# Weight tiles split in halves of their K tiles, with four half buffers, and token groups taken in the order of the K tiles

## The chip, the cores and the metric

The kernel runs on one core of one Trainium2 chip. The metric is the device time of one execution in microseconds (us), lower is better; the figure that counts is the median of several runs. The chance classes of the prediction go by 0.5%, since runs of one kernel differ by a few tenths of a per cent.

## The reference

The program is a decoder trunk with two residual layers over 512 tokens of width 2048, all in float32. Layer 0 is gated differential attention, layer 1 gated RWKV-7 time mixing.

```python
for i in range(2):                                  # layer 0, layer 1
    hn = rms_norm(x, norm_w[i])
    if i == 0:                                      # 8 heads, values of 256
        q, k, v, gate = split(hn @ da_w_in, 4)      # da_w_in 2048 x 8192
        o = causal_diff_attention(rope(rms(q)), rope(rms(k)), v, lam)
        out = (rms_norm(o) * (1 - lambda_init) * silu(gate)) @ da_w_out
    else:                                           # 32 heads of 64
        p = hn @ rw_w_in                            # 2048 x (4*2048 + 192)
        p = p + (token_shift(p) - p) * mu
        r, k, v, g, dw, da = split(p)
        y = wkv7_scan(r, decay(dw), k, v, a(da))    # S <- S*w + (S a) b + v k, y = S r
        out = (group_norm(y) + bonus) * silu(g) @ rw_w_out
    x = x + out
```

## The kernel before

**Arithmetic.** A matmul operand in float32 is split into a high part in the type float32r (a copy, which rounds) and a low part (the remainder), and a product is three matmuls: high by high, high by low, low by high (`mm3`, L114 to L119). The hidden states are held split for the whole layer (16 K tiles `hH`, `hL` of 128x512). The weights come from memory in groups: `load_w` (L73) puts 1024 columns per partition into a raw tile `wraw` (three buffers), and `split_w` (L88) makes `wh` with a copy on ScalarE (ACT, L104) and `wl` with a subtraction on VectorE (DVE, L105). `wh` and `wl` have two buffers each, so a third group can be split only when TensorE (PE) has done the last matmul of the first. `split_w` runs at a raised priority (`@urgent`).

**Layer 0.** `unit_tok` (L157) projects four blocks of 128 tokens by 512 columns: eight groups of KG = 2 K tiles, 24 matmuls in each, with the hidden states as stationary and the weights as moving operand. Within a group the order is token block by token block, save in groups marked `fine` (the first group of the kernel, whose split is also done K tile by K tile) and in a last group with work in `more`, which go K tile by K tile. The attention of the head before runs beside it in small steps (`Chain`, `tick`): after so many matmuls a step is put in. The output projections use `unit_tok` for two column blocks and then `seven` (L492), a Strassen-like form whose groups have 12 matmuls.

**Layer 1.** For each of 16 pairs of heads `unit_chan` (L883) projects one of k, g, r, v: two groups of KG = 8 K tiles by 128 columns (128x1024 again), 24 matmuls in each, K tile by K tile. So a pair takes eight groups, in the order v, k of the next pair, g of an earlier pair, r of the next pair. Three other things run beside these matmuls:

- the solve of a triangular system, `t_solve` (L1122): 31 steps of two dependent DVE instructions (`tmpl`, L1142, and `Tm`, L1144), from `LT` (L1133) to the last product (L1145); `Tm` then goes to memory and comes back as `TT` by two DMAs;
- `t_combine` (L1153): two DVE transposes of `TT` into `T1` (L1168, one per head; "T" in the profile), two runs of small matmuls `px` (L1174), copies to `X` (L1177), and two more runs of `px` (L1184). The matmuls `gp` of `gram` (L1075), whose copies to `G` (L1083) feed the next solve, stand between them;
- the scan, `scan_pair` (L1245): for each of 8 chunks a matmul `sm` (L1256), a copy to `rhs` on ACT (L1259), a matmul (L1267), a copy to `VS` on ACT (L1269), a matmul (L1274), and the next `VS` on DVE (L1278, in the first chunk L1281). Each step is put after a set number of projection matmuls.

**What sets the order.** The program is handed to a list scheduler (Tile), which fixes the order on every engine by priorities, by the set places of chain steps (`issue_after`) and by a model of durations. Engines then work strictly in that order: an instruction that waits holds up everything behind it on its engine. Buffers of a pool are taken in turn, so the scheduler also decides which instruction waits for which release.

Of the kernel before, what the change touches and what calls it, by code (L numbers as in the profile page):

```python
# [13 lines left out]
F32 = mybir.dt.float32  # L14
F32R = mybir.dt.float32r
# [8 lines left out]
P = 128  # L24
D = 2048
T = 512
KT = D // P
# [56 lines left out]
    return ld.ins  # L84


@urgent
def split_w(g, parts, kg, cols, k0, raw=None, fine=False, first=False):  # L88

    nc = g.nc  # L90
    if raw is None:
        raw = g.wraw.tile([P, kg, cols], F32, name="wraw", tag="wraw")
        load_w(g, raw, parts, k0, slice(0, kg))
    hi = g.wh.tile([P, kg, cols], F32R, name="wh", tag="wh")
    lo = g.wl.tile([P, kg, cols], F32R, name="wl", tag="wl")
    for ks in [slice(k, k + 1) for k in range(kg)] if fine else [slice(0, kg)]:
        k = k0 + ks.start
        with ExitStack() as after:
            if raw is not None and parts and k < 4:
                for ins in g.made[k - 1] if k else [g.made_prm]:  # L100
# [3 lines left out]
            nc.scalar.copy(hi[:, ks], raw[:, ks])  # L104
            nc.vector.tensor_sub(lo[:, ks], raw[:, ks], hi[:, ks].bitcast(F32))  # L105
    return hi, lo


def qk_cols(aps, h):
# [12 lines left out]
class Chain:  # L122
# [34 lines left out]
def unit_tok(g, aH, aL, parts, cols, npp=NT, more=None, late=True):  # L157

    nc = g.nc
    pts = [g.pp.tile([P, 512], F32, name="pp", tag="pp") if t < npp else  # L160
           g.ps.tile([P, 512], F32, name="pt", tag="pb", bufs=2) for t in range(NT)]
    KG = 1024 // cols
    m = None
    for k0 in range(0, KT, KG):
        raw, fine = g.first.pop(0) if g.first else (None, False)
        if fine:
            more(1, None)
        wh, wl = split_w(g, parts, KG, cols, k0, raw, fine)
        by_k = fine or more and late and k0 + KG == KT
        order = [(k, t) for k in range(KG) for t in range(NT)] if by_k else \  # L170
                [(k, t) for t in range(NT) for k in range(KG)]
        for i, (k, t) in enumerate(order):
            if more and (fine and i % 2 == 0 or i in (0, 2, 4)):
                more(1 + i // 2 if fine else k0 + (k + 1 + i % 4 // 2 if by_k else KG + i // 2), m)
# [267 lines left out]
class Rows:  # L442
# [5 lines left out]
    def __getitem__(self, k):  # L448
        return self.pairs[k][self.i]
# [3 lines left out]
KG = 2  # L453
# [143 lines left out]
def layer0(g, aps):  # L597
# [3 lines left out]
    with ExitStack() as cx:  # L601
# [46 lines left out]
        def more(n, m):  # L648
            for k in range(len(g.hH), min(n, KT)):
# [831 lines left out]
def body(ctx, tc, nc, aps):  # L1481
    g = Ctx()
# [42 lines left out]
```

## Time and profile before

| | us |
|---|---|
| median of 3 runs | 2230.39 |
| lowest and highest | 2227.97, 2237.57 |
| the profiled execution | 2223.03 |
| its span, first to last instruction | 2221.3 |
| PE busy | 2172.7 |
| DVE busy | 1405.4 |
| ACT busy | 1040.3 |

Layer 0 takes about the first 1000 us of the span, layer 1 the rest; the pairs of layer 1 run from about 1050 to 2050 us. The granted TensorE clock is full in every slice of the page. In the rows, "128x1024" is partitions by elements; a number in brackets is the idle time of the engine ahead of the instruction with what ended it; DVE, ACT and PE rows show starts that are exact and, for PE, ends that are modelled, so that on PE the distance from start to start says how long something took.

### The profile page before, as it was taken

To read this page: it belongs to the slowest core of one execution; us is meant where nothing else is said; L and a number is where in the kernel's file an instruction comes from. 1 tells how busy PE (TensorE), PEld (TensorE's weight loads), DVE (VectorE), ACT (ScalarE), POOL (GpSimd) and SP (SyncE) were. 2 spreads that over 40 slices of the span, in tenths; PEclk is the share of its full clock that TensorE was granted. 3 is DMA by queue.
4 is the path that set the end of the run, shared out by engine and by line. 5 is a ranking of instruction groups with operands and counts; after the bars stand their busy time and mean duration, and the time that the engine had idled before them with its cause. 6 is when DMAs were issued, how large, how long until landed. Compare 5 with 4: busy or idle time off the path is not lost.

```text
span 2221.3 us, 34087 instructions
## 1 busy us (share of the span) xinstructions
PE 2172.7 (98%) x12260; PEld 1754.3 (79%) x12260; DVE 1405.4 (63%) x3780; ACT 1040.3 (47%) x2118; POOL 300.3 (14%) x637
## 2 busy tenths in 40 slices
PE   9999999999999999999999999999999999999999
PEld 7888888888888888877767777777777777777887
DVE  5664636465564675475767677766667776667645
ACT  5443434344343454345555555555455555545322
POOL 0000000000000000111132212222222222231001
PEclk9999999999999999999999999999999999999999
DMA  6323232222323455644333323333333333345556
GB/s 191 97 84 97 76 105 89 92 95 77 99 82 97 145 190 194 161 108 108 86 77 77 91 75 93 83 79 91 91 91 82 87 86 77 98 136 185 170 165 121
DMA packets 296313, 240.21 MB, mean 108 GB/s; under 512 B 47792, under 2 KB 255680, under 8 KB 296144
## 3 DMA queue, kind: packets, MB, share of 16 engines
q1 hardware_dynamic: 256912, 190.13, 29.2%
q0 software_dynamic: 12384, 29.72, 6.2%
q10 hardware_dynamic: 26848, 18.18, 2.7%
q8 instruction: 97, 1.59, 0.3%
q14 instruction: 72, 0.59, 0.1%
HBM read 217.98 MB, written 19.99 MB: 107 GB/s over the span
## 4 chain that ended last, share of the span: by engine, by line
PE 70%; DVE 17%; ACT 4%; DMA 4%; issue 4%; POOL 0%; ACTq 0%; SPq 0%; DVEq 0%; POOLq 0%
PE pp L116 52%; PE pt L116 4%; DVE tmpl L1142 3%; DVE wl L105 3%; DMA td<-Tm 2%; DVE Tm L1144 2%; DMA TT<-td 1%; PE sc L116 1%; PE o L116 1%; PE sm L1267 1%; PE sm L1274 1%; DVE VS L1278 1%; PE sm L1256 1%; PE px L1174 1%; PE gp L1075 1%
## 5 line engine op out<-in xcount | busy, mean ns | idle before, releaser
L105 DVE TENSOR_TENSOR wl<-wraw,wh 128x1024 fp32r<-128x1024 f32 (+2 forms) x319 | 391.0, 1226 | 487.8 <-ACT wh L104 487.4
L104 ACT CAST wh<-wraw 128x1024 fp32r<-128x1024 f32 (+2 forms) x319 | 333.4, 1045 | 527.6 <-PE pp L116 387.9
L116 PE MATMUL pp<-wh,hH 128*128 128x512 f32 x1268 | 499.5, 394 | 0.5 <-ACT hH L869 0.3
L116 PE MATMUL pp<-wl,hH 128*128 128x512 f32 x1268 | 498.1, 393 | 0.0
L116 PE MATMUL pp<-wh,hL 128*128 128x512 f32 x1268 | 497.8, 393 | 0.1
L116 PE MATMUL pp<-hL,wh 128*128 128x512 f32 x1024 | 414.5, 405 | 0.0
L116 PE MATMUL pp<-hH,wl 128*128 128x512 f32 x1024 | 412.9, 403 | 0.0
L116 PE MATMUL pp<-hH,wh 128*128 128x512 f32 x1024 | 409.6, 400 | 0.0
L116 PEld LDWEIGHTS pp<-wh,hH 128*128 128x128 f32 x1268 | 238.3, 188 | 49.4 <-PE pp L116 0.6
L116 PEld LDWEIGHTS pp<-wh,hL 128*128 128x128 f32 x1268 | 238.2, 188 | 48.8 <-DVE hL L870 0.5
L116 PEld LDWEIGHTS pp<-wl,hH 128*128 128x128 f32 x1268 | 238.4, 188 | 46.6
L116 PEld LDWEIGHTS pp<-hH,wh 128*128 128x128 f32 x1024 | 193.1, 189 | 35.2 <-issue 1.8
L116 PEld LDWEIGHTS pp<-hL,wh 128*128 128x128 f32 x1024 | 193.1, 189 | 33.6
L116 PEld LDWEIGHTS pp<-hH,wl 128*128 128x128 f32 x1024 | 193.2, 189 | 31.9 <-issue 0.2
L1142 DVE SCALAR_TENSOR_TENSOR tmpl<-LT,Tm 128x60 f32<-128x60 f32 (+24 forms) x496 | 133.8, 270 | 9.8
L1262 POOL COPY SA<-VS 64x64 f32<-64x64 f32 x224 | 59.8, 267 | 418.3 <-DVE VS L1278 370.5
L462 POOL DMA_DIRECT2D frow<-yd x12 | 8.9, 744 | 794.4 <-DVE rs_t L67 675.1
L1144 DVE TENSOR_TENSOR Tm<-Tm,tmpl 128x60 f32<-128x60 f32 (+24 forms) x496 | 103.2, 208 | 8.0
L1259 ACT COPY rhs<-sm 64x64 f32<-64x64 f32 x256 | 52.9, 207 | 91.8 <-PE sm L1256 69.2
L1269 ACT COPY VS<-sm 64x64 f32<-64x64 f32 x256 | 52.9, 207 | 63.5 <-PE sm L1267 58.4
L1267 PEld LDWEIGHTS sm<-rhs,TT 128*128 128x128 f32 x256 | 41.8, 188 | 48.2 <-ACT rhs L1259 44.1
L1278 DVE SCALAR_TENSOR_TENSOR VS<-sm,gam,Sg 64x64 f32<-64x64 f32 x192 | 54.2, 282 | 31.6 <-PE sm L1274 27.2
(333 smaller groups left out, 3192.5 us busy)
## 6 DMA issues: line engine op xcount, KB each, us to landing
wraw<-in_rw_w_in_dram SPq DMA_DIRECT2D x128, 512.0 KB
wraw<-in_da_w_in_dram SPq DMA_DIRECT2D x254, 256.0 KB
wraw<-in_da_w_out_dram SPq DMA_DIRECT2D x26, 512.0 KB
wraw<-in_rw_w_out_dram SPq DMA_DIRECT2D x26, 512.0 KB
LT<-ltd POOLq DMA_DIRECT2D x64, 132.0 KB, 3.2
yr<-yd SPq DMA_DIRECT2D x28, 256.0 KB
frow<-yd POOLq DMA_DIRECT2D x12, 512.0 KB, 6.8
xq<-in_x_dram SPq DMA_DIRECT2D x16, 256.0 KB
```

Of the source, the lines that this page charges most:

```text
L104: nc.scalar.copy(hi[:, ks], raw[:, ks])
L105: nc.vector.tensor_sub(lo[:, ks], raw[:, ks], hi[:, ks].bitcast(F32))
L116: m = nc.tensor.matmul(out, a, b, start=s, stop=e, skip_group_check=skip)
L1075: m = nc.tensor.matmul(gp[h][:, i * P : (i + 1) * P], BK[r_, c0 + i, :, :], p.AR[r_, c0 + i, :, :], start=True, stop=True)
L1142: nc.vector.scalar_tensor_tensor(tt, LT[:, i : i + 1, i + 1 :].to_broadcast([P, s, n]), n2[:, i : i + 1], Tm[:, 0:s, i : i + 1].to_broadca ...
L1144: nc.vector.tensor_add(Tm[:, 0:s, i + 1 :], Tm[:, 0:s, i + 1 :], tt)
L1174: nc.tensor.matmul(px[hi, c * HALF : (c + 1) * HALF], p.G[lo, c, 0, h, HALF:C], T1[lo, c, :], start=True, stop=True, tile_position=(b0, b0 ...
L1259: nc.scalar.copy(rhs[r_, :], sm[r_, h * C : h * C + C])
L1262: nc.gpsimd.tensor_copy(p.SA[r_, c - 1, :], VS[r_, c, h, :])
L1267: nc.tensor.matmul(sm[:, P : P + C], both(g.TT[j % 2][:, c]), rhs[:], start=True, stop=True)
L1269: g.copied = nc.scalar.copy(VS[r_, c, h, :], sm[r_, P : P + C]).ins
L1278: g.state = nc.vector.scalar_tensor_tensor(VS[r_, c + 1, h, :], s_, p.gam[r_, c : c + 1], Sg[r_, :], ALU.mult, ALU.add)
```

## The change

`split_w` now makes two tiles of half the K tiles each instead of one (one K tile of 512 columns in layer 0, four K tiles of 128 columns in layer 1), each with its own copy and its own subtraction; a small class finds the right half when a matmul asks for K tile k. The pools `wh` and `wl` have four buffers of half the size in place of two, the same bytes. The middle groups of `unit_tok` (neither first nor last) go K tile by K tile. The old parameter `fine` of `split_w` goes, since every group is now split in halves; and the ties to the making of the first hidden states hold for the first loads alone. `wraw` and the loads are as before.

```diff
+class Halves:
+    def __init__(self, parts, n):
+        self.parts, self.n = parts, n
+    def __getitem__(self, at):
+        return self.parts[at[1] // self.n][at[0], at[1] % self.n, at[2]]
 
 @urgent
-def split_w(g, parts, kg, cols, k0, raw=None, fine=False, first=False):
+def split_w(g, parts, kg, cols, k0, raw=None, first=False):
...
-    hi = g.wh.tile([P, kg, cols], F32R, name="wh", tag="wh")
-    lo = g.wl.tile([P, kg, cols], F32R, name="wl", tag="wl")
-    for ks in [slice(k, k + 1) for k in range(kg)] if fine else [slice(0, kg)]:
-        k = k0 + ks.start
+    n = kg // 2
+    his, los = [], []
+    for k in range(0, kg, n):
+        hi = g.wh.tile([P, n, cols], F32R, name="wh", tag="wh")
+        lo = g.wl.tile([P, n, cols], F32R, name="wl", tag="wl")
...
-            nc.scalar.copy(hi[:, ks], raw[:, ks])
-            nc.vector.tensor_sub(lo[:, ks], raw[:, ks], hi[:, ks].bitcast(F32))
-    return hi, lo
+            nc.scalar.copy(hi[:], raw[:, k : k + n])
+            nc.vector.tensor_sub(lo[:], raw[:, k : k + n], hi[:].bitcast(F32))
+        his.append(hi)
+        los.append(lo)
+    return Halves(his, n), Halves(los, n)
...
-        by_k = fine or more and late and k0 + KG == KT
+        slow = more and late and k0 + KG == KT
+        by_k = fine or slow or 0 < k0 < KT - KG
...
-    g.wh = ctx.enter_context(tc.tile_pool(name="whp", bufs=2))
-    g.wl = ctx.enter_context(tc.tile_pool(name="wlp", bufs=2))
+    g.wh = ctx.enter_context(tc.tile_pool(name="whp", bufs=4))
+    g.wl = ctx.enter_context(tc.tile_pool(name="wlp", bufs=4))
```

The scheduler's order changes with it. On ACT and DVE 341 instructions each are added; PE, POOL and SP issue as many as before, POOL in the same order. Three places of a pair in the middle of layer 1 are shown (the order repeats from pair to pair there). The changed kernel's line numbers are 16 higher from L172 on, and its copy and subtraction stand at L117 and L118; a matmul on plain float32 counts once here and as two records in the profile.

On ACT, from the two scalings `BK` of the keys to a copy to `rhs` of the scan; before:

```order
L1038 ACTIVATE BK<-th_14966,prm_bk_b_1158,prm_bk_s_1155 128x8x64
L1259 COPY rhs<-sm 64x64 x2
L1038 ACTIVATE BK<-th_14966,prm_bk_b_1164,prm_bk_s_1161 128x8x64
L1028 ACTIVATE E<-m 128x8
L1269 COPY VS<-sm 64x64 x2
L1044 ACTIVATE k_15107<-mixk,prm_kk 128x512
L1029 ACTIVATE E<-l 128x8x64
L878 CAST sHx<-k_15107 128x512
L1030 ACTIVATE l<-l 128x512
L1214 COPY VS<-pt 64x4x64 x4
L104 CAST wh<-wraw 128x1024
L1259 COPY rhs<-sm 64x64 x2
```

And now, the same stretch:

```order
L1054 ACTIVATE BK<-th_15920,prm_bk_b_1228,prm_bk_s_1225 128x8x64
L1275 COPY rhs<-sm 64x64 x2
L117 CAST wh<-wraw 128x512
L1044 ACTIVATE E<-m 128x8
L1054 ACTIVATE BK<-th_15920,prm_bk_b_1234,prm_bk_s_1231 128x8x64
L1285 COPY VS<-sm 64x64 x2
L1045 ACTIVATE E<-l 128x8x64
L1060 ACTIVATE k_16069<-mixk,prm_kk 128x512
L1046 ACTIVATE l<-l 128x512
L894 CAST sHx<-k_16069 128x512
L1230 COPY VS<-pt 64x4x64 x4
L117 CAST wh<-wraw 128x512
```

The next row of the changed kernel is the same copy to `rhs` (L1275), with another half behind it. The whole group that stood ahead of that copy has become one half ahead of it and one behind it, and half of a group stands further up. A second whole group, some ten rows ahead of this stretch, has become one half as well.

On DVE, the end of the solve; before:

```order
L1142 SCALAR_TENSOR_TENSOR tmpl<-LT,Tm 128x8
L1311 TENSOR_REDUCE s_15239<-Y 128x4
L1144 TENSOR_TENSOR Tm<-Tm,tmpl 128x8
L1311 TENSOR_REDUCE s_15239<-Y 128x4
L1145 TENSOR_TENSOR Tm<-Tm,LT 128x256
L1312 TENSOR_SCALAR s_15239<-s_15239 128x4 x2
```

And now:

```order
L1158 SCALAR_TENSOR_TENSOR tmpl<-LT,Tm 128x8
L1160 TENSOR_TENSOR Tm<-Tm,tmpl 128x8
L1161 TENSOR_TENSOR Tm<-Tm,LT 128x256
L1327 TENSOR_REDUCE s_16209<-Y 128x4 x2
L1328 TENSOR_SCALAR s_16209<-s_16209 128x4
L118 TENSOR_TENSOR wl<-wraw,wh 128x512
```

A few rows further down, the two transposes of `TT`; before:

```order
L908 SCALAR_TENSOR_TENSOR mixr<-pp,prmin_rw_mu_dram,mixr 128x511
L1059 TENSOR_TENSOR AR<-mixr,E 128x8x64
L1168 STREAM_TRANSPOSE T_15268<-TT_9335 64x256
L1060 SCALAR_TENSOR_TENSOR mixr<-mixr,prm_hrk,f 128x512
L1168 STREAM_TRANSPOSE T_15268<-TT_9335 64x256
```

And now:

```order
L924 SCALAR_TENSOR_TENSOR mixr<-pp,prmin_rw_mu_dram,mixr 128x511
L1075 TENSOR_TENSOR AR<-mixr,E 128x8x64
L1184 STREAM_TRANSPOSE T_16238<-TT_10025 64x256
L1076 SCALAR_TENSOR_TENSOR mixr<-mixr,prm_hrk,f 128x512
L118 TENSOR_TENSOR wl<-wraw,wh 128x512
L1184 STREAM_TRANSPOSE T_16238<-TT_10025 64x256
```

The two reductions `s` have moved behind the end of the solve, and a half subtraction now stands between the two transposes. Inside the solve, from its first row to its last, eight halves stand where four whole ones stood (in the first three pairs and the last, seven where three stood).

On PE, the combining of the solve's result; before:

```order
L1174 MATMUL px<-T_15268,G_14631 32x32 x8
L1075 MATMUL gp<-AR,BK 128x128 x6
L1174 MATMUL px<-T_15268,G_14631 32x32 x8
L1075 MATMUL gp<-AR,BK 128x128 x10
L1184 MATMUL px<-TT_9335,X 32x32 x16
```

And now:

```order
L1190 MATMUL px<-T_15517,G_14852 32x32 x8
L1091 MATMUL gp<-AR,BK 128x128 x2
L1190 MATMUL px<-T_15517,G_14852 32x32 x8
L1091 MATMUL gp<-AR,BK 128x128 x14
L1200 MATMUL px<-TT_10026,X 32x32 x16
```

The second run of `px` has moved up past four of the `gp`; on ACT both copies to `X` now stand ahead of all four copies to `G`, where two of those stood between them. Further on, the second matmul of the scan's first chunk (L1267) and the third of its second chunk (L1274) have each moved up past two projection matmuls.

More of the change, by code (lines that the diff above doesn't have):

```diff
@@ L84, in load_w @@
     return ld.ins
+class Halves:
[3 more added lines that the diff above has]
+        return self.parts[at[1] // self.n][at[0], at[1] % self.n, at[2]]
 @urgent
-def split_w(g, parts, kg, cols, k0, raw=None, fine=False, first=False):
+def split_w(g, parts, kg, cols, k0, raw=None, first=False):
     nc = g.nc
+    held = raw is not None and parts
     if raw is None:
@@ L93, in split_w @@
         load_w(g, raw, parts, k0, slice(0, kg))
-    hi = g.wh.tile([P, kg, cols], F32R, name="wh", tag="wh")
-    lo = g.wl.tile([P, kg, cols], F32R, name="wl", tag="wl")
-    for ks in [slice(k, k + 1) for k in range(kg)] if fine else [slice(0, kg)]:
-        k = k0 + ks.start
+    n = kg // 2
[3 more added lines that the diff above has]
+        lo = g.wl.tile([P, n, cols], F32R, name="wl", tag="wl")
         with ExitStack() as after:
-            if raw is not None and parts and k < 4:
-                for ins in g.made[k - 1] if k else [g.made_prm]:
+            if held and k0 + k < 4:
+                for ins in g.made[k0 + k - 1] if k0 + k else [g.made_prm]:
                     after.enter_context(g.tc.issue_after(ins))
```

4 lines of the change are left out of this document (2 added, 2 removed).

## Prediction

> **What bounds the kernel now.** I read the page's engine lines first, then who TensorE (PE) waits for over the whole span, then windows, then the rows of one pair of layer 1. On the page (share of the span, instructions) PE is the engine to beat:
>
> ```profile
> PE 2172.7 (98%) x12260; PEld 1754.3 (79%) x12260; DVE 1405.4 (63%) x3780; ACT 1040.3 (47%) x2118; POOL 300.3 (14%) x637
> ```
>
> ```profile
> PE sm L1267 <- ACT rhs L1259: 11.2, 15, 0.9
> PE px L1174 <- DVE T L1168: 9.4, 14, 2.0
> PE px L1184 <- ACT X L1177: 7.0, 11, 0.6
> ```
>
> ```profile
> PE z L116 <- DVE wl L105: 0.2, 1, 0.2
> ```
>
> The three rows are PE's longest waits from 1100 to 2020 us (total, times, longest); the single one is from the waits of the whole span, the only one there of a matmul for a weight split. So the split itself is never late; what the change can win or lose is what its copies and subtractions do to other work in the same queues. Where that is, the windows say (us, then busy us of PE, PEld, DVE, ACT, POOL, clock, DMA):
>
> ```profile
> 200.00:300.00 100.00, 100.00 (x481) 83.40 (x480) 56.79 (x165) 39.82 (x78) 0.00 (x0) 1.00 0.28 90
> 1400.00:1500.00 100.00, 96.16 (x585) 74.93 (x584) 73.05 (x217) 55.80 (x129) 25.06 (x56) 1.00 0.30 79
> 1473.40:1509.20 35.80, 34.72 (x218) 26.97 (x217) 33.32 (x114) 20.55 (x50) 6.81 (x19) 1.00 0.30 83
> ```
>
> In layer 0 PE has no gap at all, in layer 1 it loses nearly 4 us of 100. The third window is one solve of layer 1: DVE is busy for 33.32 of 35.80 us there. That solve closes a loop, and PE waits for it once a pair:
>
> ```profile
> 1450.63 0.66 PE L1174 MATMUL px<-T,G 32*32 32x32 f32 x16 [0.94 <-DVE T L1168]
> ...
> 1452.09 0.69 PE L1174 MATMUL px<-T,G 32*32 32x32 f32 x16
> 1452.70 1.39 PE L1075 MATMUL gp<-AR,BK 64*128 64x128 f32 x20
> 1454.73 0.43 PE L1184 MATMUL px<-TT,X 32*32 32x32 f32 x8 [0.64 <-ACT X L1177]
> ...
> 1515.03 0.66 PE L1174 MATMUL px<-T,G 32*32 32x32 f32 x16 [0.39 <-DVE T L1168]
> ```
>
> From px to px a pair takes 1515.03 − 1450.63 = 64.40 us. Two paths lead from one px to the next, and the longer sets the period: PE's own work, and the loop px, gp, scan, solve, two DMAs, transpose, px. PE's wait at px, 9.4/14 = 0.67 us on average, is the lead of the second path over the first. So a gain on the loop counts up to that wait and what PE's own path gives back as well; a loss on the loop counts in full.
>
> **The change part by part.** *Price of a half.* The rows by shape (count, busy us, mean ns):
>
> ```profile
> L105 DVE TENSOR_TENSOR wl<-wraw,wh 128x1024 fp32r<-128x1024 f32 x313 | 385.8, 1232 | 484.3 <-ACT wh L104 483.9 <-ACT VS L1269 0.3
> L425 DVE TENSOR_TENSOR hL<-yr,hH 128x512 fp32r<-128x512 f32 x28 | 18.3, 684 | 1.9 <-ACT hH L424 1.9
> L104 ACT CAST wh<-wraw 128x1024 fp32r<-128x1024 f32 x313 | 328.8, 1051 | 521.3 <-PE pp L116 387.9 <-issue 67.5 <-PE pt L116 36.4
> L104 ACT CAST wh<-wraw 128x512 fp32r<-128x512 f32 x2 | 1.2, 613 | 2.9 <-DMA wraw<-in_da_w_in_dram 2.9
> ```
>
> Two halves cost 2·684 − 1232 = 136 ns more on DVE and 2·613 − 1051 = 175 ns more on ACT; for the 341 added instructions that is 46 and 60 us of busy time. In layer 0 it lies beside PE, which has no gap there, with DVE at 57% and ACT at 40%: I take 0. If that cover were gone, the wait would have to appear at the splits, where today 0.2 us stand.
>
> *Order by K tile in layer 0's middle groups.* The same matmuls run, only the accumulating tile changes after three instead of six. `seven` already goes K tile by K tile (its `pt`), layer 0's units mostly do not:
>
> ```profile
> L116 PE MATMUL pp<-wh,hH 128*128 128x512 f32 x1268 | 499.5, 394 | 0.5 <-ACT hH L869 0.3 <-DVE gs L328 0.2
> L116 PE MATMUL pt<-wh,hH 128*128 128x512 f32 x120 | 47.1, 393 | 0.0
> ```
>
> A matmul takes 394 ns in the one and 393 in the other: 0, with bounds of 1 ns either way for some 2300 matmuls, 2 us. Twice as many waits on `wh` and `wl` reach PE; a satisfied one has no row of its own, so I take 0, and 1 us as its bound (the same 1 ns for 682 waits; no gain can come of a wait).
>
> *The solve (DVE).* What counts is the distance to the next start:
>
> ```profile
> 1496.98 0.72 DVE L879 TENSOR_TENSOR sLx<-k,sHx 128x512 fp32r<-128x512 f32 x1
> 1497.62 0.28 DVE L1142 SCALAR_TENSOR_TENSOR tmpl<-LT,Tm 128x66 f32<-128x66 f32 x1
> 1497.82 1.21 DVE L105 TENSOR_TENSOR wl<-wraw,wh 128x1024 fp32r<-128x1024 f32 x1
> 1498.95 0.21 DVE L1144 TENSOR_TENSOR Tm<-Tm,tmpl 128x66 f32<-128x66 f32 x1
> ...
> 1508.05 0.42 DVE L1311 TENSOR_REDUCE s<-Y 128x4 f32<-128x256 f32 x1
> 1508.39 0.16 DVE L1144 TENSOR_TENSOR Tm<-Tm,tmpl 128x8 f32<-128x8 f32 x1
> 1508.46 0.41 DVE L1311 TENSOR_REDUCE s<-Y 128x4 f32<-128x256 f32 x1
> 1508.79 0.41 DVE L1145 TENSOR_TENSOR Tm<-Tm,LT 128x256 f32<-128x256 f32 x1
> ```
>
> A subtraction of 512 columns holds DVE for 0.64 us, one of 1024 for 1.13 us, a reduction for 0.34 and 0.33 us. By the order in a middle pair eight halves replace four wholes, 8·0.64 − 4·1.13 = +0.60 us, and the two reductions go behind the last product, −0.67 us: together −0.07 us. In the first three pairs and the last, seven halves replace three wholes and no reduction goes: 7·0.64 − 3·1.13 = +1.09 us each.
>
> The reductions now lie in the time in which `Tm` travels. Behind them DVE has 0.67 us more and, of its two halves ahead of `mixr`, 0.15 us more to do before the first transpose, and that transpose waited 0.37 us for its DMA; but `mixr` no longer stands behind a whole copy on ACT:
>
> ```profile
> 1510.38 1.05 ACT L104 CAST wh<-wraw 128x1024 fp32r<-128x1024 f32 x1 [5.88 <-PE pp L116]
> 1511.46 0.69 ACT L907 ACTIVATE mixr<-pp,omu 128x512 f32<-128x512 f32 x1
> ```
>
> ```profile
> 1511.46 1.22 DVE L105 TENSOR_TENSOR wl<-wraw,wh 128x1024 fp32r<-128x1024 f32 x1 [1.39 <-ACT wh L104]
> ```
>
> DVE idled 1.39 us for that copy, which waited for PE to release a whole group; the halves ahead of `mixr` are of parts released earlier. 1.39 covers 0.82. The first transpose stays bound by its DMA.
>
> *The start of the solve.* It stands on DVE behind the scan's second update of `VS`:
>
> ```profile
> 1472.17 1.23 DVE L105 TENSOR_TENSOR wl<-wraw,wh 128x1024 fp32r<-128x1024 f32 x1 [4.61 <-ACT wh L104]
> 1473.32 0.59 DVE L1278 SCALAR_TENSOR_TENSOR VS<-sm,gam,Sg 64x64 f32<-64x64 f32 x2
> 1473.94 0.18 DVE L1133 TENSOR_SCALAR LT<-LT 128x32 f32<-128x32 f32 x1
> ...
> 1476.70 0.28 DVE L1278 SCALAR_TENSOR_TENSOR VS<-sm,gam,Sg 64x64 f32<-64x64 f32 x1 [0.66 <-PE sm L1274]
> ```
>
> ```profile
> 1472.53 0.49 PE L1274 MATMUL sm<-VS,BKT 128*128 128x128 f32 x2
> ...
> 1476.10 0.38 PE L1274 MATMUL sm<-VS,BKT 128*128 128x128 f32 x1
> ```
>
> After 1472.53 `VS` came 0.79 us late because a whole subtraction was in front; after 1476.10 it came after 0.60. The halves there can start earlier, since the first half of the group before is released at its middle: −0.2 us (bounds −0.2 and 0). The matmul at 1472.53 also stands two projection matmuls earlier, 2·0.23 = −0.45 us, of which I leave 0.05 for waits it meets: −0.4 us (bounds −0.45 and +0.1, if `VS` on ACT, now behind two halves, is late).
>
> *The combining.* Before, `X` waited behind two copies to `G` and PE idled 0.64 us; now both copies to `X` come first, and that wait goes. Late next is the second transpose. It now stands behind a half subtraction, queued in front of it for 0.64 us:
>
> ```profile
> 1515.55 0.44 DVE L1168 STREAM_TRANSPOSE T<-TT 64x256 f32<-64x256 f32 x1
> ```
>
> It would end at 1515.55 + 0.64 + 0.44 = 1516.63, and px comes some 0.05 us later (as L1267 at 1492.49 after its `rhs`, below), 1.65 us after the first px. PE arrives after four gp instead of twelve, at about 0.6 + 4·0.07 = 0.9 us, and waits some 0.75 us. The second run takes 0.61 us (1452.09 to 1452.70) and 28 gp of 0.07 us (1.39/20) follow: L1184 comes at 1.65 + 0.61 + 2.0 = 4.26 us after the first px instead of 4.10. Net +0.2 us (bounds 0, if the half finds an idle slot, and +0.6, if its copy on ACT, which waits for PE's last r matmul behind `mixr`, is late; queued behind that copy are the copies to `G` and `X`). SP's four loads of `TT` stand behind the same loads as before but in one early pair; POOL's order is unchanged.
>
> Loop of a middle pair: −0.07 − 0.2 − 0.4 + 0.2 = **−0.5 us** (−0.7 to +0.6).
>
> *PE's own path.* Its longest single wait in a pair is for `rhs`:
>
> ```profile
> 1490.95 1.04 ACT L104 CAST wh<-wraw 128x1024 fp32r<-128x1024 f32 x1
> 1492.02 0.42 ACT L1259 COPY rhs<-sm 64x64 f32<-64x64 f32 x2
> ```
>
> ```profile
> 1492.49 0.43 PE L1267 MATMUL sm<-rhs,TT 128*128 128x64 f32 x2 [0.84 <-ACT rhs L1259]
> ```
>
> Now one half stands ahead of `rhs` instead of a whole, one instead of a whole further up, and half of a third has come in between: 3·0.6 − 2·1.05 = −0.3 us. With +0.2 from the combining, about −0.1: PE's path keeps its length, and the 0.5 us lie within the 0.67 us that PE waits, so they count.
>
> Sum against the profiled execution (2223.03 us for a span of 2221.3): twelve middle pairs −0.5·12 = −6.0; the first three and the last +1.09 each, less 0.6 (the start's −0.2 and −0.4) in the three that have a scan beside their solve, +2.6; layer 0 and `seven` −0.2: −3.6 us, or 2219.4. That execution lies 7.4 us under the median shown, so the median becomes **2227 us**.
>
> [...]
>
> **The rivals.** *Gain given back.* The loop shortens, but PE's path grows by as much (the 0.75 us wait for the second transpose in front of PE, waits in the re-ordered scan steps): 0 a pair, and the early pairs' +2.6: 2233. For it: waits moved, not removed, in the combining. *Both paths shorten.* The reductions, the start and `rhs` give all that their bounds allow, −0.7 a pair, halves fill 0.3 of the 2.48 us in which DVE idles in the solve (35.80 − 33.32), and the early pairs lose nothing: −1.0·12, 2218. For it: 0.67 + 0.84 us of PE's waits a pair hang on ACT or DVE being held by wholes. *Slower.* In the solve, where DVE has little room, each half waits for its own copy on ACT, which now comes in eight pieces between other copies. It decides from 0.06 us of wait per half (0.5/8); at 0.2 us a half the loop is 1.6 − 0.5 = 1.1 us longer a pair, 13 us, with the early pairs 16 us: 2246. Against it: ACT is busy only 20.55 of 35.80 us there. *The change does nothing* (halves land where wholes stood) is ruled out by the order.
>
> **How the numbers follow.** Forecast 0.45, given back 0.2, both shorten 0.22, slower 0.13. The loop's bounds, −0.7 to +0.6 over twelve pairs with the other terms, give 2224 to 2240; the case in which both shorten is to be held as well, with some room for what its bounds leave out: 2215 to 2240. Over 0.5% is 11 us, about what a measurement of this kernel tells from no change: faster 0.21 (both shorten, nearly all), slower 0.11, within 0.68.
>
> **What will show it.** Right: PE's wait for X at L1184 gone, one for the second T in its place; `rhs` row below 0.84 us; period px to px near 63.9 us; solve window's DVE busier. Wrong: a row in which PE waits for `wl` or `wh`, DVE idle for `wh` within the solve, or any change of PE's pace in layer 0.

## The result, and the profile after

The changed kernel took 2230.45 us in the median of 12 runs (2225.84 to 2238.86), the kernel before beside it 2229.49 (12 runs, 2224.06 to 2240.66): a ratio of 1.0002, with a 95% interval of 0.9983 to 1.0021. Nothing that can be measured was won or lost. One run each of e8, of e9 and of the kernel before took 3393, 3353 and 6420 us; these three are left out of every figure below. The profiled execution of the change has a span 9.9 us longer than that of before, and the first line to read is the clock. Span and mean granted TensorE clock of the core, first of the change, then of before:

```profile
core 0: 2231.2 us, clock 0.990
```

```profile
core 0: 2221.3 us, clock 1.000
```

The engine line of the page of the change (busy us, share of the span, instructions):

```profile
PE 2190.8 (98%) x12260; PEld 1769.9 (79%) x12260; DVE 1441.8 (65%) x4121; ACT 1092.8 (49%) x2459; POOL 311.3 (14%) x637
```

The 341 added instructions cost DVE 36 and ACT 52 us of busy time (46 and 60 forecast). Who TensorE (PE) waits for from 1100 to 2020 us in the change (total, times, longest):

```profile
PE px L1190 <- DVE T L1184: 12.4, 22, 2.1
PE sm L1283 <- ACT rhs L1275: 4.0, 15, 0.4
PE sm L1290 <- ACT VS L1285: 1.4, 3, 0.9
PE sm L1272 <- DVE VS L1294: 0.4, 2, 0.3
```

The wait for `rhs` has shrunk from 11.2 to 4.0 us, the wait for `X` (7.0 us) is gone, the waits for `T` have become more (14 to 22) and together 3 us longer. No row names `wl` or `wh`, and in 14 of the 16 solves DVE doesn't idle for `wh` (0.2 us in each of the first two). PE thus waits some 10 us less, and yet the kernel isn't faster. The middle of layer 1, two solves and the first 500 us of steady work in layer 0 in windows (us, then busy us and instructions of PE, PEld, DVE, ACT, POOL, the clock, DMA share, GB/s):

```profile
1260.00:2040.00 780.00, 764.78 (x5067) 601.25 (x5067) 546.94 (x1667) 427.78 (x1028) 200.19 (x434) 0.98 0.35 93
```

```profile
1482.35:1516.65 34.30, 33.91 (x215) 26.55 (x215) 31.92 (x112) 21.53 (x55) 7.76 (x18) 1.00 0.25 71
```

```profile
200.00:700.00 500.00, 500.00 (x2396) 416.88 (x2395) 293.64 (x902) 212.71 (x471) 0.00 (x0) 1.00 0.28 91
```

In layer 0 PE does 2396 matmuls in 500 us, before the change 2395, at a full clock. In layer 1 the clock is 0.98, where before had 1.00. PE's rows of one middle pair of the change, from one px to the next, without the rows that the argument doesn't use:

```profile
1784.09 0.66 PE L1190 MATMUL px<-T,G 32*32 32x32 f32 x16 [0.28 <-DVE T L1184]
1784.67 0.49 PE L1091 MATMUL gp<-AR,BK 64*128 64x128 f32 x4
1785.70 0.69 PE L1190 MATMUL px<-T,G 32*32 32x32 f32 x16 [0.53 <-DVE T L1184]
1786.32 1.83 PE L1091 MATMUL gp<-AR,BK 64*128 64x128 f32 x28
1788.08 1.09 PE L1200 MATMUL px<-TT,X 32*32 32x32 f32 x32
...
1847.47 0.69 PE L1190 MATMUL px<-T,G 32*32 32x32 f32 x16
```

This pair takes 1847.47 − 1784.09 = 63.38 us, where before took 64.40. The px starts of the change are 1263.54, 1326.83, 1391.17, 1459.61, 1523.40, 1588.76, 1653.67, 1717.40, 1784.09, 1847.47, 1911.53 and 1975.15. Eleven distances: seven of 63.29 to 64.34, in the mean 63.75, and four longer ones of 68.44, 65.36, 64.91 and 66.69 us. Before, the same eleven have a mean of 64.53. So seven pairs gained 0.78 us each, 5.5 us, and four lost 7.3 us. A fall of the clock to 0.50 lies in each of these four (for 10.24, 3.41, 3.41 and 6.83 us), and in none of the seven. What sets the four apart is seen in steps of 3.41 us around the px at 1717.40 (same columns as above):

```profile
1713.71:1717.12 3.41, 3.37 (x15) 2.44 (x13) 2.19 (x4) 1.06 (x2) 0.73 (x5) 1.00 0.14 22
1717.12:1720.53 3.41, 2.60 (x52) 2.36 (x54) 1.81 (x4) 1.37 (x4) 0.00 (x0) 1.00 0.68 171
1720.53:1723.95 3.42, 3.42 (x51) 3.05 (x48) 0.00 (x0) 2.79 (x6) 0.52 (x1) 0.50 0.00 0
1723.95:1727.36 3.41, 3.41 (x9) 2.51 (x8) 0.00 (x0) 1.63 (x4) 1.25 (x2) 0.50 0.10 14
1727.36:1730.77 3.41, 3.41 (x17) 2.83 (x17) 0.69 (x1) 1.20 (x4) 0.00 (x0) 1.00 0.51 117
```

After a step in which PE was busy 2.60 of 3.41 us, with px and gp and no projection matmul, the clock is 0.50 for two steps: in the second of them 9 matmuls pass, where 17 pass at full clock. Before, the same place of a pair looks so:

```profile
1709.71:1713.12 3.41, 2.77 (x62) 2.42 (x59) 0.00 (x0) 2.46 (x6) 0.00 (x0) 1.00 0.43 126
1713.12:1716.54 3.42, 3.42 (x35) 2.78 (x30) 0.00 (x0) 3.33 (x7) 1.78 (x2) 1.00 0.13 19
```

PE was busy for 2.77 us, and the clock stays. The pair quoted further up, from 1784.09 us, has its two waits as well, but there a boundary of the same steps parts them, and the clock stays too:

```profile
1781.97:1785.39 3.42, 2.91 (x29) 2.05 (x27) 2.27 (x5) 1.23 (x2) 0.61 (x5) 1.00 0.37 66
1785.39:1788.80 3.41, 3.10 (x70) 2.94 (x71) 0.26 (x1) 2.32 (x7) 0.00 (x0) 1.00 0.46 131
```

The steps ahead of the four falls held 0.81 to 1.46 us of idle PE, with both waits in one step. Two other steps at a px of these pairs held 0.82 and 0.83 us, and the clock stayed, so where exactly the line runs is not known. In the profile of the change the clock falls six times in layer 1, for 41.0 us together; in the quoted profile of before it never falls there.

### The profile page after: what moved, and what is told of

Same layout as the page of the kernel before. It is cut to its first block, busy times and chain, and to the rows that moved or that the text cites. A ratio compares the mean times of both kernels' runs of the same rounds, so it can differ in the third digit from the quotient of the medians.

```text
span 2231.2 us, 35111 instructions
## 1 busy us (share of the span) xinstructions
PE 2190.8 (98%) x12260; PEld 1769.9 (79%) x12260; DVE 1441.8 (65%) x4121; ACT 1092.8 (49%) x2459; POOL 311.3 (14%) x637
## 5 line engine op out<-in xcount | busy, mean ns | idle before, releaser
L118 DVE TENSOR_TENSOR wl<-wraw,wh 128x512 fp32r<-128x512 f32 (+1 forms) x636 | 437.9, 692 | 498.2 <-ACT wh L117 494.8
L117 ACT CAST wh<-wraw 128x512 fp32r<-128x512 f32 (+1 forms) x636 | 392.9, 619 | 597.1 <-PE pp L131 477.9
L131 PE MATMUL pp<-hH,wh 128*128 128x512 f32 x1024 | 414.1, 404 | 0.0
L1275 ACT COPY rhs<-sm 64x64 f32<-64x64 f32 x256 | 52.5, 205 | 87.4 <-PE sm L1272 61.0
L1281 POOL TENSOR_SCALAR Sg<-SA,gam 128x64 f32<-128x64 f32 x96 | 79.9, 832 | 9.4
```

The lines of the kernel that those rows point to most:

```text
L117: nc.scalar.copy(hi[:], raw[:, k : k + n])
L118: nc.vector.tensor_sub(lo[:], raw[:, k : k + n], hi[:].bitcast(F32))
L131: m = nc.tensor.matmul(out, a, b, start=s, stop=e, skip_group_check=skip)
L1275: nc.scalar.copy(rhs[r_, :], sm[r_, h * C : h * C + C])
L1281: nc.gpsimd.tensor_scalar(Sg[:], p.SA[:, c - 1, :], p.gam[:, c : c + 1], None, ALU.mult)
```

## The experiments

**Theory A.** The change shortens the loop of a pair as forecast, and pays it back in clock: it has put PE's two waits of a pair (0.33 to 0.93 us for the first T in the four pairs that fell, 0.53 us for the second) into one short stretch with hardly any projection matmuls, and after such a stretch TensorE runs at half clock for 3.41 us or a multiple (3.41 to 10.24 us in the profile of the change). **Rival B:** the clock falls come alike in both kernels, whatever stands around px, and nothing was gained. **Rival C:** layer 0 loses what layer 1 gains.

The runs of all kernels in one table. "Full clock" is an estimate: the mean time less 1.84 us for each 0.001 of mean clock lost. The 1.84 is the slope of a straight line through 97 runs of the kernel before (2222.3 us at a clock of 1.000). Ratios are to the runs of before beside them. The other kernels' own lines are less sure (the 12 runs of the change alone give 1.68 in place of 1.84, and 2216.6 us), so a us or two of a "full clock" can be the estimate's.

| kernel | runs | median us | ratio (95%) | mean clock | full clock, us |
|---|---|---|---|---|---|
| before, all runs | 97 | 2231.1 | | 0.9953 | 2222.3 |
| before once more (e1) | 12 | 2233.2 | 1.0000 (0.9981–1.0018) | 0.9948 | 2222.2 |
| the change | 12 | 2230.5 | 1.0002 (0.9983–1.0021) | 0.9913 | 2215.1 |
| e2, layer 1 only | 6 | 2255.4 | 1.0096 (1.0072–1.0120) | 0.9933 | 2242.1 |
| e3, layer 0 only | 6 | 2253.4 | 1.0095 (1.0070–1.0120) | 0.9963 | 2247.4 |
| e4, turned first | 12 | 2223.1 | 0.9965 (0.9946–0.9984) | 0.9944 | 2213.0 |
| e5, filled | 12 | 2229.8 | 1.0007 (0.9994–1.0019) | 0.9942 | 2219.0 |
| e6, px apart | 4 | 2277.2 | 1.0215 (1.0192–1.0239) | 0.9805 | 2239.5 |
| e7, layer 1 only, b | 12 | 2233.8 | 1.0024 (1.0008–1.0039) | 0.9915 | 2218.7 |
| e8, layer 0 only, b | 7 | 2236.5 | 1.0041 (1.0017–1.0065) | 0.9936 | 2225.5 |
| e9, mid turned | 11 | 2226.2 | 0.9980 (0.9959–1.0001) | 0.9924 | 2213.6 |
| e10, first px later | 10 | 2220.3 | 0.9951 (0.9933–0.9970) | 0.9964 | 2213.8 |
| e11, before, px later | 12 | 2230.9 | 0.9999 (0.9982–1.0016) | 0.9948 | 2221.5 |
| e12, turns behind y | 6 | 2221.1 | 0.9943 (0.9925–0.9962) | 0.9952 | 2211.4 |

**e1, the kernel before once more**, to see the clock of its runs. No edit.

> The kernel before, unchanged, so that the granted clock of each of its runs is seen. In the profile of the change TensorE's clock falls to half in six stretches of layer 1 (3.41 to 10.24 us each, 41 us together), in that of before in none; over the 12 runs of the change time falls with the mean clock by 1.68 us for 0.001 of clock and would be 2217 us at a clock of 1.000, where before took 2223. Theory A (the change gains some 6 us and pays them back in clock): the runs of before lie on a line through 2223 us at 1.000, with a mean clock near 0.996 ((2229.5 - 2223) / 1680), higher than the 0.991 of the change. Rival B (the clock dips belong to both alike, the profile of before was a lucky one): mean clock 0.991 as for the change, and the runs of before lie 5 us or more under a line of that slope through 2223 us.

The mean clock was 0.9948, and of all 97 runs of before 0.9953, with a line through 2222.3 us: theory A's two numbers. Before has falls too (this profile has a clock of 0.993), but fewer. At full clock the change is 2222.3 − 2215.1 = 7.2 us faster; it runs at 0.0040 less clock, which costs 0.0040 / 0.001 · 1.84 = 7.4 us. The two add up to the difference of the mean times by construction; what is measured is that the clock is lower and that the runs lie under the line. With the slope of the change's own runs the gain is 5.7 us. Rival B fails: the profiles say the same, as from 1260 to 2040 us those with halves in layer 1 and the order of the change (the change, e7, e2) have four, four and two falls, and those with layer 1 as before (before, e1, e3, e8, e11) none, one, none, none and none.

**e2 and e3, one layer each.** `split_w` keeps its whole form in one of the layers, and the pools are opened per layer:

```diff
-    g.wh = ctx.enter_context(tc.tile_pool(name="whp", bufs=4))
-    g.wl = ctx.enter_context(tc.tile_pool(name="wlp", bufs=4))
     for n, layer in ((4, layer0), (2, layer1)):
-        with tc.tile_pool(name="pp", bufs=n, space=PSUM) as g.pp, \
+        g.whole = layer is layer0        # layer1 in the other kernel
+        bufs = 2 if g.whole else 4
+        with tc.tile_pool(name="whp", bufs=bufs) as g.wh, tc.tile_pool(name="wlp", bufs=bufs) as g.wl, \
+                tc.tile_pool(name="pp", bufs=n, space=PSUM) as g.pp, \
```

> Halves in layer 1 alone; layer 0 has whole splits, two buffers and its old order of matmuls. Theory A: layer 0 is worth nothing, so all is as with the whole change: 2230 us (2227 to 2233), clock 0.990 to 0.994 with dips that begin within 4 us of a px, undisturbed pairs of 63.3 to 64.0 us. Rival C (halves in layer 0 cost time there, by the added copies and subtractions): 2224 us or less, with the first pair 5 us earlier than with the whole change.

> The other part alone: halves, four buffers and the order by K tiles in layer 0, whole splits in layer 1. Theory A: as before the change in both numbers: 2229.5 us (2226 to 2232), mean clock as the runs of the kernel before, pairs of 64.3 to 64.6 us. Rival C: 2235 us or more.

Both missed by over 20 us, and the reason is not the change. Layer 0 from 200 to 700 us in e2, which has the whole splits of before there:

```profile
200.00:700.00 500.00, 500.00 (x2349) 409.22 (x2348) 277.81 (x809) 194.62 (x380) 0.00 (x0) 1.00 0.28 90
```

PE does 2349 matmuls in place of 2395, at full clock and without a gap; e3 is the same. The split tiles had moved, since their pools now came behind a small one. e7 and e8 repeat both with the small pool opened behind them, so that the tiles lie where they were:

```diff
+                tc.tile_pool(name="small", bufs=3) as g.small, \
-    g.small = ctx.enter_context(tc.tile_pool(name="small", bufs=3))
```

> Halves in layer 1 alone once more, with the tiles of the splits at the addresses that they have in the change. In the two runs with one layer each a matmul of layer 0 took 233 ns from start to start in place of 227, in both alike, with split tiles that had been moved. Theory A with the address as the cause of that: layer 0 at 227 ns, 2230 us (2227 to 2234), clock 0.990 to 0.994, pairs of 63.3 to 64.1 us without a dip. Rival (two kinds of splits in one kernel cost the 6 ns themselves): 2252 us again.

> Halves, four buffers and the order by K tiles in layer 0 alone, with the tiles at the addresses that they have in the change. Theory A: layer 0 is worth nothing, so 2230 us (2226 to 2234) at a mean clock of 0.995 as before the change, pairs of 64.3 to 64.6 us. Rival C (layer 0's added copies or its order cost time): 2235 us or more. Rival (two kinds of splits cost it): 2252 us again.

The same stretch in e7:

```profile
200.00:700.00 500.00, 500.00 (x2393) 416.73 (x2392) 282.81 (x822) 199.43 (x390) 0.00 (x0) 1.00 0.28 91
```

The instruction order of e7 is that of e2 on every engine, so where the pools lie had alone cost those 20 us. e7 then shows both sides of the change, its low clock (0.9915) and its faster pairs (those without a fall 63.4 to 64.3 us). e8 has the pairs of before (64.2 to 65.1 us) and at full clock 2225.5 us, not less than before. Some of that is the experiment's own: opening the pools per layer makes PE wait where layer 1 begins:

```profile
PE pp L145 <- ACT wh L117: 1.8, 1, 1.8
```

in e8, 1.4 us in e7. So most of the lower clock lies in layer 1, and most of the gain (5.0 of the 7.2 us at full clock, e7's wait set aside). Layer 0 is not settled: e8's 2236.5 us lie where rival C put them (2235 or more), about half of its distance to before being a lower clock (0.9936) and the rest 3.2 us at full clock, 1.8 of them that wait. Nor do the parts add up: e7 is 3.6 us under before at full clock and e8 3.2 us over it; less the two waits that makes 3.6 us of gain, where the whole change has 7.2. Against rival C stand layer 0's windows, with the same number of matmuls.

**e4, the second transpose ahead of the half.** The last half of a v group is tied behind it:

```diff
-            nc.vector.transpose(T1[r_], TT[r_, :, h, 0:HALF])
+            g.turned = nc.vector.transpose(T1[r_], TT[r_, :, h, 0:HALF]).ins
...
+            if tie and k:
+                after.enter_context(g.tc.issue_after(tie))
             nc.vector.tensor_sub(lo[:], raw[:, k : k + n], hi[:].bitcast(F32))
```

> The change, with the last half subtraction of each v group tied behind the second transpose of TT, so that no half stands between the two transposes. Both theories expect the second transpose 1.1 us after the first in place of 1.70, and PE's wait of 0.53 us for it in the middle pairs to go, most of it given back at the first px in pairs that the loop binds. Theory A with the dips caused by the idle and near-idle TensorE around px: fewer dips, clock 0.994 or more, 2224 to 2227 us. Rival B (dips come whatever stands around px): clock 0.991, 2227 to 2230 us.

DVE, then PE, at one px of e4:

```profile
1704.00 0.43 DVE L1187 STREAM_TRANSPOSE T<-TT 64x256 f32<-64x256 f32 x1 [1.44 <-DMA TT<-td]
1704.37 0.70 DVE L1079 SCALAR_TENSOR_TENSOR mixr<-mixr,prm_hrk,f 128x512 f32<-128x512 f32 x1
1705.10 0.44 DVE L1187 STREAM_TRANSPOSE T<-TT 64x256 f32<-64x256 f32 x1
```

```profile
1704.58 0.66 PE L1193 MATMUL px<-T,G 32*32 32x32 f32 x16 [0.60 <-DVE T L1187]
1705.17 0.48 PE L1094 MATMUL gp<-AR,BK 64*128 64x128 f32 x2
1705.59 0.69 PE L1193 MATMUL px<-T,G 32*32 32x32 f32 x16
```

The second transpose comes 1.10 us after the first, PE doesn't wait for it, and e4 is 0.35% faster than before, although the tie made PE wait 8.5 us for one `wl` in the first pair. The clock is 0.9944: up from the change's 0.9913, as theory A wants, but just at its mark; the time, 2223.1 us, is a us under its range. The tie also altered the first pairs, which e9 takes out.

**e5, the waits filled.** Two matmuls without use in the wait for the second transpose:

```diff
+        if before and c0 == 0:
+            for _ in range(2):
+                m = nc.tensor.matmul(gp[1][:], g.hH[0][:, 0:P], g.hH[1][:], start=True, stop=True)
```

and the px run of the second head is placed behind the first two gp. From 1262 to 2038 us the order on PE, DVE and ACT is otherwise that of the change; in the first three pairs and behind the last one the scheduler moved other work too.

> The change, with two matmuls of 128x512 more in each of 14 pairs, whose result is overwritten unused: they stand between the first run of px and the second, where TensorE waits 0.53 us for the second transpose; both px runs, the gp between them and the order on the other engines stay. Theory A (TensorE's clock is halved for the next 3.41 us when a stretch of 3.41 us on a fixed grid held more than some 0.6 us of idle TensorE and hardly any projection matmul, and the change has put two waits, 0.4 and 0.53 us, into one such stretch): idle there falls to 0.5 us, the dips in the middle pairs go, the mean clock rises from 0.991 to 0.995 or more, and the time falls to 2223 to 2227 us although TensorE has 28 x 0.227 = 6 us more to do. Rival B (the dips have another cause, TensorE's load or the chip's state): clock 0.991, time 2230 to 2237 us.

PE around a px of e5, and the middle of layer 1:

```profile
1719.91 0.66 PE L1199 MATMUL px<-T,G 32*32 32x32 f32 x16 [0.57 <-DVE T L1191]
1720.50 0.73 PE L1091 MATMUL gp<-hH 128*128 128x512 f32 x2
1721.16 0.49 PE L1095 MATMUL gp<-AR,BK 64*128 64x128 f32 x4
1721.59 0.69 PE L1199 MATMUL px<-T,G 32*32 32x32 f32 x16
```

```profile
1260.00:2040.00 780.00, 770.73 (x5197) 603.38 (x5196) 555.13 (x1694) 430.03 (x1035) 201.59 (x437) 1.00 0.35 95
```

No fall is left from 1260 to 2040 us (four in the change, the clock there 0.98); three remain in the first pairs, 34 us together. The mean clock rose by 0.0029, worth 5.3 us, and the added work cost 3.9 us at full clock (2219.0 − 2215.1). 2229.8 us is slower than expected by 3 us and the clock, 0.9942, a little short of 0.995, so the time alone doesn't tell theory A from rival B (from 2230 us); the clock does. The filling isn't free, but more work gave no longer time. That what PE does between the two px runs decides the falls in the middle pairs is hereby shown, within what one profile of each can show: nothing else in the order was changed there. Whether it is the idle time or the lack of wide matmuls, e5 doesn't part, since it changed both. The 0.6 us of idle in theory A is the author's estimate; no run shows where that mark lies.

**e6, px apart from gp**, with projections between the two runs:

```diff
     for h, b0, lo, hi in blocks:
+        if h:
+            yield 3
         for c in range(NC_):
...
-            stage_v(g, j, p, proj(2, j, behind=(18, behind)))
+            stage_v(g, j, p, proj(2, j, behind=(21, behind)))
```

> The change, with the matmuls gp ahead of the first px, three projection matmuls between the two runs of px and some twenty between the second run and the px that need X. Theory A: no stretch of 3.41 us is left without projection matmuls and with 0.6 us of idle in the middle pairs, so no dips there and a mean clock of 0.995 or more; the wait for the second transpose goes. The scan starts some 20 x 0.227 = 4.5 us later in its pair, which the time has room for or not: 2215 to 2235 us, 2222 if it has. Rival B: clock 0.991 as with the change, whatever the period.

A miss, and a clear one. The scheduler put all gp ahead of the first px, and there they wait for the step behind the output of an earlier pair:

```profile
PE gp L1091 <- DVE s L1330: 9.6, 11, 1.4
```

```profile
1406.57 0.46 PE L1091 MATMUL gp<-AR,BK 64*128 64x128 f32 x2 [1.22 <-DVE s L1330]
1407.57 1.17 PE L1091 MATMUL gp<-AR,BK 64*128 64x128 f32 x14 [0.55 <-DVE yc L1331]
1408.67 1.06 PE L1192 MATMUL px<-T,G 32*32 32x32 f32 x16
```

1.22 + 0.55 = 1.77 us of wait with no projection near, and at 1408.53 the clock falls to 0.50, as at 1340.26; from 1260 to 2040 us it is 0.96 in the mean (0.9805 over the runs, the lowest of all). That fits theory A, with more of its cause in a kernel that was meant to have less, but it is no test of it; the period is longer at full clock too.

**e9, e10, e12: a version that beats both; e11, its control.** e9 is e4 with the tie from the third combining on. e10 starts the first px of all later, since PE stands still for it at half clock (in the change for 1.98 of the 5.68 us that it waits there, at 0.50 from 1092.48 us):

```diff
-                    pairs[0].chain.wait += 28
+                    pairs[0].chain.wait += 52
...
-    yield GAP_X
+    yield GAP_X if j else 4
```

e11 puts the like (40 and 8) into the kernel before. e12 is e10 with both transposes of the first pair tied behind `y`, and the places of that pair's steps set anew.

> The change, with the last half of a v group behind the second transpose as in the run with the transposes together, but only from the third combining on; there the tie made TensorE wait 8.5 us for a wl in the first pair. Theory A: middle pairs with at most one dip (idle next to px down from 0.9 to 0.5 us), the first pairs as in the change (5.7 us wait and a dip of 7 to 14 us): clock 0.993 to 0.995, 2219 to 2225 us, and a line through 2208 to 2213 us at full clock. Rival B (the faster time of that run came from its first pairs): 2228 to 2231 us.

> The run before it, with the first px of the first pair 24 projection matmuls (5.4 us) later and its px on X 15 matmuls sooner after that, so that TensorE projects while the first T is on its way. Theory A: the wait of 5.7 us at the first px and the dip behind it go, clock 0.996 or more, 2211 to 2218 us. Rival (the first pairs are bound by their loop, so the wait comes back at the px of the second pair): only the dip goes or moves, 2217 to 2223 us.

> A control: the kernel before, with the first px of the first pair 12 projection matmuls (2.7 us) later and its px on X 11 matmuls sooner after that; nothing of the change. It tells how much of the run beside it the change has no part in. Theory A: the wait of 2.7 to 3.3 us at the first px goes and its dip with it, clock 0.997 or more, 2223 to 2227 us. Rival (the wait comes back at the next px): 2228 to 2231 us.

> The run with the first px later, in which TensorE still stood still for 5.8 us in the first pair, now for sLx, which DVE had queued behind the first transpose of TT and its wait of 5.3 us for the DMA. Here both transposes of the first pair are tied behind y, so that mixv, sLx and y come first. Theory A (the idle stretch and the clock dip behind it both go): 2212 to 2217 us at a mean clock of 0.997 or more, TensorE's longest wait in the first pair under 1.5 us. Rival (two half subtractions stand behind the transposes, so the wait comes back as one for wl): a wait for wl of 2 us or more, 2218 to 2221 us.

e9 was slower than expected (2226.2 us): at full clock it is 0.6 us above its range (2213.6), but the clock is 0.9924, and its profile has falls in each of the first three pairs. Its interval reaches 1.0001, so the second transpose put right in the middle pairs alone is no gain that can be told from nothing. e10 is clearly under the kernel before, 0.9951 of it, at a clock of 0.9964, but 2 us over theory A's range and within its rival's. Its wait had not gone:

```profile
PE pt L1014 <- DVE sLx L897: 5.8, 1, 5.8
```

DVE had queued `sLx` behind the first transpose, which waits 5.34 us for its DMA. e12 takes that away (PE's longest wait in the first pair is 1.5 us), and stays at the time of e10, 2221.1 us against 2220.3: faster at full clock (2211.4), but at 0.9952, not the 0.997 that was expected. Theory A had put it at 2212 to 2217 us; its rival is not seen either, since no wait for `wl` came. Six runs do not tell whether its clock is really lower than e10's. e11, without the change, gained nothing: 0.9999, its rival's time. It isn't the clean control it was meant to be, since PE still waits 2.9 us at that px, now for `y`:

```profile
PE px L1174 <- DVE y L1199: 2.9, 1, 2.9
```

What the runs show is this: e9 and e10 take the same time at full clock (2213.6 and 2213.8 us), and the first px later raised the mean clock by 0.0040, which is the whole of the 7 us between their mean times. How it did so with the wait still there was not traced.

## Why the prediction was right, point by point

The forecast was 2227 us and no difference, the result 2230.45 and no difference. The loop moved the way that was forecast; what brought the time back was not in the sum. That the number came out is in part luck: two misses, a gain some twice the forecast's and a loss of clock of the same size, cancelled.

- **Layer 0: 0.** Right. 2396 against 2395 matmuls in 500 us, and the last weight subtraction ahead of the first solve starts at 1056.28 us in place of 1056.53.
- **The start of the solve and the combining: −0.4 us** (−0.2 − 0.4 + 0.2). Measured from px to the `LT` row, the first of the solve on DVE: 23.31 us before (1450.63 to 1473.94); in the change 1784.09 to

```profile
1806.84 0.18 DVE L1149 TENSOR_SCALAR LT<-LT 128x32 f32<-128x32 f32 x1
```

  that is 22.75 us, −0.56. The wait for `X` is gone and one of 0.53 us for the second T has come (0.75 forecast). The px on X starts 1788.08 − 1784.09 = 3.99 us after the first, before 4.10: the net is −0.1 us, where +0.2 was forecast.
- **The solve: −0.07 us.** Too small. From that row to the last product,

```profile
1841.13 0.42 DVE L1161 TENSOR_TENSOR Tm<-Tm,LT 128x256 f32<-128x256 f32 x1
```

  it is 34.29 us, before 34.85 (1473.94 to 1508.79): −0.56. The reductions gave their 0.67 us. By starts on DVE, eight halves took 4.90 us and four wholes 4.54: +0.36, where 8 · 0.64 − 4 · 1.13 = +0.60 was forecast. And the 62 steps themselves, from start to next start, fell from 14.64 to 14.32 us. The window's DVE is busy 31.92 of 34.30 us, 93%, as before (33.32 of 35.80): "busier" was wrong. The first three pairs and the last were to lose 1.09 us each in their solves; measured in the same way they changed by +0.86, +0.80, −0.05 and +0.21.
- **The first transpose "stays bound by its DMA".** Right, but the DMA became slower in most pairs. The write of `Tm` and the next POOL row, which waits for it:

```profile
1778.11 0.99 POOL L1162 DMA_DIRECT2D td<-Tm  x1 [1.99 <-DVE Tm L1161]
1781.85 0.31 POOL L1151 MEMSET Tm<- 128x256 f32 x1 [2.75 <-DMA td<-Tm]
```

```profile
1509.51 0.99 POOL L1146 DMA_DIRECT2D td<-Tm  x1 [2.54 <-DVE s L1312]
1512.60 0.31 POOL L1135 MEMSET Tm<- 128x256 f32 x1 [2.10 <-DMA td<-Tm]
```

  3.74 us in the change, 3.09 before (second fence). By the same two rows most middle pairs of the change show 3.5 to 4.3 us, four of them 3.1, the end of the pair quoted above among these. This term of about +0.5 us was missing, and on average it eats what the solve gained beyond the forecast.
- **The period: 63.9 us, −0.5.** Measured 63.75 in pairs at full clock, −0.78, with the bounds at −0.7 and +0.6: just outside.
- **PE's own path.** The wait for `rhs` fell to

```profile
1825.24 0.44 PE L1283 MATMUL sm<-rhs,TT 128*128 128x64 f32 x2 [0.26 <-ACT rhs L1275]
```

  0.26 from 0.84 us, −0.58 where −0.3 was forecast. At three of the twelve px starts listed above PE has no wait left (1263.54, 1653.67 and 1847.47 us): there its own path is the longer one.
- **The sum.** −3.6 us forecast, −7.2 us at full clock by the estimate above (−5.7 by the change's own runs): the direction and, as far as e7 shows, the place right, half to two thirds of the size.
- **The step that failed**, though the number held, is the last one: "that execution lies 7.4 us under the median shown, so the median becomes 2227 us". It carried the distance from profile to median over as if it were the same for both kernels. The distance is clock: the quoted execution of before had a clock of 1.000, its 97 runs have 0.9953 in the mean, and 0.0047 are 8.6 us. The change runs at 0.9913, where the distance is 16 us. The prediction saw a wait move from in front of X to in front of the second T and priced it at +0.2 us; it did not ask what stood around it. Before, the two waits of a pair are 4.1 us apart (1450.63 and 1454.73); in the change they are 1.6 us apart.

Of the rivals, "gain given back" came nearest in its number (2233) and named the wait for the second transpose; its mechanism, PE's path made longer by waits, is not the one found. "Slower" is refuted: no half waits long enough in the solve, since it became shorter.

In the first pairs the change waits 5.68 us at the first px,

```profile
1094.46 1.06 PE L1190 MATMUL px<-T,G 32*32 32x32 f32 x16 [5.68 <-DVE T L1184]
```

before 2.67 us; by 1263.54 us it is 7.1 us behind the profile of before, with 17 us at half clock among them. How much of these 7.1 us is clock and how much loop was not taken apart.

## What to carry to other kernels

Before pricing a moved wait, look at what TensorE does within some three us on either side of it: here two short waits among small matmuls (0.33 and 0.53 us) were followed by 6.83 us at half clock, and that pair took 66.69 us where the others took 63.75; the price shows only in the windows' clock column. A profiled execution with a clock of 1.000 was not a median one here; take the mean clock of several runs, compare kernels at equal clock, and report both numbers. When an edit frees an engine at one place, see what it queues at the next: here a half slipped between two transposes. Moving it behind them in all pairs (e4) gave 0.35% against the kernel before, in the middle pairs alone (e9) 0.20%, which can't be told from nothing.

## What the runs showed of the hardware that was not expected

- **The clock falls on a grid.** In the profile of the change the six falls of layer 1 begin at 1092.48, 1150.50, 1392.85, 1525.97, 1590.83 and 1720.53 us, which are 17, 71, 39, 19 and 38 steps of 3.41 us apart, and last one to three such steps (3.41 to 10.24 us), at 0.50. In the profiles of all these kernels 54 falls were counted between 1000 and 2060 us, each from a boundary of one such grid per profile, for one to five steps (3.41 to 17.07 us). In the middle pairs the step ahead held 0.5 us or more of idle PE, mostly with both px runs (1.2 us of 32x32 matmuls); in the first pairs about 1.3 us or more of idle (3.41 and 1.51 us in the change). It isn't a full rule: before, three steps of the first pairs with 1.68 to 1.72 us of idle kept the clock, steps with the 0.64 us wait for X did, and so did, in most middle pairs, a step with the 0.84 us wait for `rhs`. Where the grid lies differs from run to run (boundaries at 1091.89 us before, counted back from its one fall, at 2221.71 us behind the last instruction, 1093.24 in e1, 1092.48 in the change). Two profiles of the kernel before, with the same order on PE, DVE, ACT and POOL, show what this does at the first px: in the quoted one (first two rows) a boundary parts the wait and the clock stays, in e1's (last two) all of it lies in one step and the clock falls:

```profile
1088.48:1091.89 3.41, 1.70 (x8) 1.08 (x6) 0.84 (x2) 1.09 (x2) 0.90 (x6) 1.00 0.87 201
1091.89:1095.31 3.42, 2.46 (x30) 1.88 (x31) 1.99 (x3) 0.62 (x1) 3.37 (x6) 1.00 0.79 194
1089.83:1093.24 3.41, 0.48 (x4) 0.07 (x3) 0.56 (x2) 0.00 (x0) 1.88 (x8) 1.00 0.68 176
1093.24:1096.65 3.41, 3.41 (x22) 2.65 (x22) 1.42 (x2) 0.62 (x1) 2.58 (x4) 0.50 0.97 235
```

  That this is why the same kernel takes 2222 us at a clock of 1.000 and 2241 us at 0.990 is likely, but was not traced run by run. The step ahead of a fall need not be idle throughout: PE was busy 2.60 of 3.41 us ahead of the fall at 1720.53.
- **The place of a tile counts.** With the pools of the split tiles opened in another place (e2), layer 0 did 2349 instead of 2395 matmuls in 500 us without a gap, 2%, or 213 ns against 209 ns for a matmul of any size; e7, with the order of e2 and the tiles back in their place, did 2393. Why, no run here shows.
- **The write of `Tm`** (128 KB, issued by POOL) takes 3.1 us to the next POOL row in most pairs before and 3.5 to 4.3 in most pairs after. In the change DVE runs the same instructions beside a write of 3.1 and one of 3.7 us, so it isn't those; other traffic is a guess that was not tried.
